# A two-layer hybrid decoder on one core: the instruction order taken from the scheduler's timeline model in place of its list model

## The chip, the cores and the metric

The kernel runs on one core of one Trainium2 chip. The metric is the device time of one execution in microseconds (us); the runs shown are of the same program on the same kind of chip, and the figure compared is their median. Matrix work runs on TensorE (PE in the profile, its weight loads PEld), elementwise work on VectorE (DVE), ScalarE (ACT) and GpSimd (POOL), and SyncE (SP) issues most DMAs.

## The reference

Two decoder layers over 512 tokens of width 1024, float32, each of them three residual steps with a layer norm behind each:

```
x <- LN(alpha*x + 0.5*SwiGLU_1(x))
x <- LN(alpha*x + W_o concat[DiffAttn | StickBreakingAttn | GatedDeltaNet](x W_in))
x <- LN(alpha*x + 0.5*SwiGLU_2(x))
```

The SwiGLU steps have a hidden width of 2816. The mixer in the middle has three parts: differential attention (4 heads, two softmaxes of 32-wide queries and keys each), stick-breaking attention (4 heads of 64, whose weights come from a reverse cumulative sum over the keys), and a gated delta rule (4 heads of 128). The delta rule cuts the sequence into chunks, solves a unit lower triangular system per chunk, and then carries a 128x128 state from chunk to chunk:

```
sol = lax.linalg.triangular_solve(t_mat, rhs, left_side=True, lower=True, unit_diagonal=True)
v_new = u_i - einsum(w_i, state)
out   = einsum(q_i * exp(g_i), state) + einsum(a_i, v_new)
state = state * exp(g_last) + einsum(k_i * exp(g_last - g_i), v_new)
```

## The kernel before, in words

Everything is held feature-major, 128 features on the partitions and the 512 tokens along the free axis. A projection is a sum over 8 (or 22) blocks of 128x128 weights. To keep float32 accuracy with a faster matmul, weights and activations are split into a high and a low part, and `mm3` (lines 100 to 107) issues three matmuls per block: L103 high by high, L104 high weights by low activations, L105 low weights by high activations. Such a matmul of 512 columns is the unit of the bulk work; it is called a *filler* below wherever it stands between the steps of a chain that is made of other, smaller instructions. Weights stream in eight blocks at a time (L81, tile `wraw`), and `Stream.get` makes the two parts on ACT (L89, `whi`) and on DVE or POOL (L90, `wlo`).

Per layer the program is `ffn`, `mixer`, `ffn`. Each of them ends in a layer norm: `Norm.add` gathers sums, L179 transposes them on PE, DVE computes the mean and the inverse deviation (`ln_yn`), and L206 transposes those back on PE, after which the next stage's inputs can be made.

The mixer is where many small chains meet:

- `project_v`, then for the four delta heads projections, convolution and products (L537 is the last of these on PE).
- `triangle(h)` for each head: L615 spreads the decay sums on PE, DVE and ACT make the lower triangle (L625), SP stores it to DRAM (L627); L630 and L633 make `intra`.
- `base`: SP loads the diagonal 16x16 blocks of all heads (L644), DVE inverts them in 30 dependent steps (L652, L654), and SP stores them (L655, L657) and loads them back as full tiles (L660 `XT`, L662 `inv`).
- `double(h)`: PE L670, ACT L672, PE L675, DVE L676, PE L679, ACT L680. It makes 32-wide inverted blocks of 16-wide ones.
- `join(h, m)` for m = 32 and 64: PE L690, ACT L693, PE L697, DVE L699, and for m = 32 PE L704 and ACT L705. Each step waits for the one ahead of it.
- `operands(h)`: PE transposes L710 and L715, DVE L712 and L717.
- `state`: for two pairs of heads and four chunks in turn `scan`: PE L725, DVE L727, PE L731, DVE L733, PE L738, DVE L741 or L744 (the new state), and the output on PE L749, L750 and ACT L792. The two pairs take turns, and a pair's next L725 needs its new state. `emit` and L776 finish two chunks.
- Attention, of small units: scores on PE (L878, L879, into tile `psc`, which has two buffers), softmax work on DVE and ACT (L915 to L938, L466), transposes L902, copy L904, values L907, and per pair of heads a closing normalization (L946 to L964) with transposes L970.
- The attention's queries and keys come from `project_qk` (L826 to L847): a 24-matmul projection, then SP DMAs (L846, `kqv<-kqv`) that lay the parts of each head out on the partitions that L878 reads.

All of it is written one stage after another. What stands beside what on an engine is not written by hand: the framework's scheduler takes the program's instructions and their dependencies, models the run, and emits one fixed order per engine. Each engine then executes its own list strictly in that order, so an instruction that waits holds up all that is behind it on that engine, SP's DMA issues included. The program gives a few hints (`g.after`, which adds an order between two instructions without a wait), and those stay. The core of the projection:

```
nc.tensor.matmul(out=out, lhsT=whi, rhs=xhi, start=first, stop=False)
nc.tensor.matmul(out=out, lhsT=whi, rhs=xlo, start=False, stop=False)
nc.tensor.matmul(out=out, lhsT=wlo, rhs=xhi, start=False, stop=last)
```

and one head's first half of `join` (a pair of blocks per corner):

```
nc.tensor.matmul(out=pt[hi, c, lo], lhsT=LTs[h][lo, c, hi], rhs=X[h][lo, c, lo], ...)
nc.scalar.copy(out=Y[hi, :, lo], in_=pt[hi, :, lo])
nc.tensor.matmul(out=pt[lo, c, hi], lhsT=Y[hi, c, lo], rhs=XT[h][hi, c, hi], ...)
nc.vector.tensor_tensor(out=XT[h][lo, :, hi], in0=XT[h][lo, :, hi], in1=pt[lo, :, hi], ...)
```

## Time and profile before

| what | value |
|---|---|
| time, three runs | 2253.29, 2254.13, 2255.03 us; median 2254.13 us |
| profiled execution | 2255.08 us, of which the profile's span is 2252.1 us |
| mean granted clock of TensorE | 0.978 |
| PE busy | 2141.5 us (95%) |
| PEld, DVE, ACT, POOL busy | 1792.2, 1153.2, 886.4, 346.7 us |
| HBM read, written | 189.64 MB, 6.83 MB |

The span runs from the first to the last recorded instruction; the 3.0 us between span and time lie around it. The profiled execution is 0.95 us above the median of the runs. Two layers follow one another: the first mixer lies between about 400 and 770 us, the second between about 1520 and 1890 us, and the rest is SwiGLU. A wait in the profile is idle time of an engine ahead of an instruction, with the instruction that released it. A granted clock of 1.00 stands for TensorE's level of 2.4 GHz, and 0.50 would be the level of 1.2 GHz throughout; a mean in between says how the stretch was shared between the two.

### The profile page before, as it was taken

Reading aid. Unit: us, or ns where it says so; the run is one execution under the profiler, and the core shown is the slowest. Engines: PE = TensorE matmul, PEld = TensorE weight load, DVE = VectorE, ACT = ScalarE, POOL = GpSimd, SP = SyncE. Lnnn points to the kernel's source line nnn. Section 1 sums busy time; section 2 is a strip of 40 time slices with the busy share of each in tenths; the row PEclk is TensorE's granted clock in tenths of the full one; section 3 lists DMA queues with packets and bytes.
Section 4 is the critical chain, followed back from the end, with each engine's and each line's share of the span. In section 5 each row is a group of like instructions: output and inputs, shape, how many; then the busy total and the mean of one; then the engine's idle time right before and its main releaser. Section 6 shows DMA issues by size and latency. Waiting matters only on the chain.

```text
span 2252.1 us, 29920 instructions
## 1 busy us (share of the span) xinstructions
PE 2141.5 (95%) x11382; PEld 1792.2 (80%) x11382; DVE 1153.2 (51%) x2347; ACT 886.4 (39%) x1755; POOL 346.7 (15%) x295
## 2 busy tenths in 40 slices
PE   8999999997988999999999999999989889999997
PEld 7888889876767888888888888898768668888886
DVE  4533436455687843333563334274566788333426
ACT  4333324545554533332443333155454635333313
POOL 1100011442113500000130000024511144000010
PEclk9999999999998999999999999999999889999998
DMA  6433323335221233332333333233442213333322
GB/s 186 128 94 97 97 75 104 94 97 135 76 67 47 84 104 100 96 94 75 113 103 96 100 94 94 66 104 103 113 101 76 76 48 103 94 95 100 96 66 94
DMA packets 89742, 213.08 MB, mean 95 GB/s; under 512 B 21840, under 2 KB 36208, under 8 KB 89600
## 3 DMA queue, kind: packets, MB, share of 16 engines
q1 hardware_dynamic: 81696, 183.27, 26.8%
q10 hardware_dynamic: 6912, 25.17, 3.7%
q0 software_dynamic: 992, 2.75, 0.7%
q8 instruction: 89, 1.46, 0.3%
q14 instruction: 53, 0.43, 0.1%
HBM read 189.64 MB, written 6.83 MB: 87 GB/s over the span
## 4 chain that ended last, share of the span: by engine, by line
PE 79%; DVE 12%; DMA 3%; ACT 2%; issue 2%; SPq 1%; POOL 1%; ACTq 0%; POOLq 0%; DVEq 0%
PE pd L104 23%; PE pd L103 23%; PE pd L105 23%; DMA wraw<-in_w 2%; DVE wlo L90 2%; PE po L907 1%; DVE x L212 1%; ACT whi L89 1%; DVE lt L166 1%; DVE at L937 1%; DMA kqv<-kqv 1%; PE psc L878 1%; DVE x L220 1%; PE pt L902 1%; DVE x L163 1%
## 5 line engine op out<-in xcount | busy, mean ns | idle before, releaser
L89 ACT CAST whi<-wraw 128x512 fp32r<-128x512 f32 x692 | 423.1, 620 | 990.8 <-PE pd L104 798.6
L90 DVE TENSOR_TENSOR wlo<-wraw,whi 128x512 fp32r<-128x512 f32 x580 | 431.0, 750 | 640.3 <-ACT whi L89 628.1
L103 PE MATMUL pd<-x,whi 128*128 128x512 f32 (+1 forms) x1888 | 714.6, 379 | 6.6 <-ACT x L1169 6.1
L104 PE MATMUL pd<-x,whi 128*128 128x512 f32 (+1 forms) x1888 | 715.6, 379 | 1.7 <-POOL x L231 1.1
L105 PE MATMUL pd<-x,wlo 128*128 128x512 f32 (+1 forms) x1888 | 713.3, 378 | 3.1 <-DVE wlo L90 3.1
L103 PEld LDWEIGHTS pd<-x,whi 128*128 128x128 f32 x1888 | 357.1, 190 | 70.9 <-ACT x L1169 6.1
L105 PEld LDWEIGHTS pd<-x,wlo 128*128 128x128 f32 x1888 | 357.6, 189 | 66.4 <-DVE wlo L90 3.3
L104 PEld LDWEIGHTS pd<-x,whi 128*128 128x128 f32 x1888 | 357.6, 189 | 66.3 <-POOL x L231 3.0
L103 PE MATMUL pd<-hhi,whi 128*128 128x512 f32 (+1 forms) x880 | 307.7, 350 | 0.0
L104 PE MATMUL pd<-hlo,whi 128*128 128x512 f32 (+1 forms) x880 | 307.6, 350 | 0.0
L105 PE MATMUL pd<-hhi,wlo 128*128 128x512 f32 (+1 forms) x880 | 307.2, 349 | 0.0
L90 POOL TENSOR_TENSOR wlo<-wraw,whi 128x512 fp32r<-128x512 f32 x112 | 151.9, 1360 | 297.8 <-ACT whi L89 214.2
L168 POOL TENSOR_TENSOR lt<-lt 128x512 f32<-128x512 f32 x26 | 39.2, 1509 | 1016.2 <-ACT lt L165 1012.1
L103 PEld LDWEIGHTS pd<-hhi,whi 128*128 128x128 f32 x880 | 165.4, 188 | 24.4
L105 PEld LDWEIGHTS pd<-hhi,wlo 128*128 128x128 f32 x880 | 165.4, 188 | 24.2
L104 PEld LDWEIGHTS pd<-hlo,whi 128*128 128x128 f32 x880 | 165.4, 188 | 24.1
L258 DVE TENSOR_TENSOR lt<-pd,lt 128x512 f32<-128x512 f32 x88 | 60.4, 690 | 112.6 <-PE pd L105 111.2
L134 POOL TENSOR_TENSOR x<-x 128x512 f32<-128x512 f32 x48 | 74.1, 1581 | 74.1 <-DVE ams L957 70.6
L515 DVE SCALAR_TENSOR_TENSOR kqv<-pd,conv,kqv 128x511 f32<-128x511 f32 (+2 forms) x54 | 40.3, 747 | 60.4 <-ACT kqv L513 59.4
L260 DVE TENSOR_TENSOR hlo<-lt,hhi 128x512 fp32r<-128x512 f32 x88 | 67.1, 765 | 6.2
L231 POOL TENSOR_TENSOR x<-x 128x256 fp32r<-128x256 f32 x60 | 45.9, 766 | 152.1 <-ACT x L229 148.3
L165 ACT ACTIVATE lt<-x 128x256 f32<-128x256 f32 (+1 forms) x58 | 29.5, 512 | 100.0 <-DVE x L163 99.8
(307 smaller groups left out, 2300.0 us busy)
## 6 DMA issues: line engine op xcount, KB each, us to landing
wraw<-in_w SPq DMA_DIRECT2D x300, 512.0 KB, 3.5
wraw<-in_w ACTq DMA_DIRECT2D x48, 512.0 KB, 3.6
kqv<-kqv SPq DMA_DIRECT2D x128, 64.0 KB, 2.0
kqv<-kqv SPq DMA_DIRECT2D x48, 128.0 KB, 3.8
scr<-zero POOLq DMA_DIRECT2D x2, 1032.0 KB, 11.4
x<-in_xT SPq DMA_DIRECT2D x8, 256.0 KB, 5.9
scr<-inv SPq DMA_DIRECT2D x8, 256.0 KB, 3.4
XT<-scr SPq DMA_DIRECT2D x8, 256.0 KB, 5.2
```

The source lines that it names most:

```text
L89: nc.scalar.copy(out=hi, in_=r)
L90: (eng or self.eng or nc.vector).tensor_tensor(out=lo, in0=r, in1=hi.bitcast(F32), op=ALU.subtract)
L103: nc.tensor.matmul(out=out, lhsT=whi, rhs=xhi, start=first, stop=False)
L104: nc.tensor.matmul(out=out, lhsT=whi, rhs=xlo, start=False, stop=False)
L105: nc.tensor.matmul(out=out, lhsT=wlo, rhs=xhi, start=False, stop=last)
L134: i = g.nc.gpsimd.tensor_tensor(out=t, in0=xhi.bitcast(F32), in1=xlo.bitcast(F32), op=ALU.add)
L165: nc.scalar.activation(out=sq[:, r], in_=t[:, r], func=AF.Square)
L168: eng.tensor_tensor(out=self.acc2[:, r], in0=self.acc2[:, r], in1=sq[:, r], op=ALU.add)
L231: eng.tensor_tensor(out=xlo[:, r], in0=t[:, r], in1=xhi[:, r].bitcast(F32), op=ALU.subtract)
L258: nc.vector.tensor_tensor(out=sg, in0=pu, in1=sg, op=ALU.mult)
L260: nc.vector.tensor_tensor(out=hlo, in0=sg, in1=hhi.bitcast(F32), op=ALU.subtract)
L515: nc.vector.scalar_tensor_tensor(out=y[:, s:], in0=p[:, :T - s], scalar=wc[:, 3 - s:4 - s], in1=y[:, s:], op0=ALU.mult, op1=ALU.add)
```

## The change

One argument is added where the kernel is built. The program, its tiles, its buffers and its hints stay as they are; the scheduler's model of the run, by which it chooses which instruction to emit next, is another.

```
-    with tile.TileContext(nc) as tc, ExitStack() as ctx:
+    with tile.TileContext(nc, schedule_with_timeline_sim=True) as tc, ExitStack() as ctx:
```

Both orders hold the same instructions. Of PE's 10860 instructions 4022 stand at another place, nearly all of them in the two mixers and around the layer norms; the bulk of the SwiGLU stages is in the same order. Three places follow, with the order of one engine before and after; "x8" behind a row stands for eight such instructions in a row.

**SP in the first mixer, around the stores and loads of `base`.** `scr_98` to `scr_100` are the three DRAM scratch tensors, `kqv<-kqv` the layout DMAs of L846. Before:

```order
L644 DMA blk<-scr_98 128x16x16
L846 DMA kqv<-kqv 64x512 x6
L655 DMA scr_99<-blk 128x16x16
L657 DMA scr_100<-blk 128x16x16
L846 DMA kqv<-kqv 64x512 x2
L660 DMA XT<-scr_99 128x4x128
L662 DMA inv<-scr_100 128x4x128
```

Behind these rows come the other three pairs of L660 and L662, and then four more L846 of this form. Now:

```order
L627 DMA scr_98<-inv 128x4x128
L644 DMA blk<-scr_98 128x16x16
L846 DMA kqv<-kqv 64x512 x5
L655 DMA scr_99<-blk 128x16x16
L657 DMA scr_100<-blk 128x16x16
L846 DMA kqv<-kqv 64x512 x2
L660 DMA XT<-scr_99 128x4x128 x2
L662 DMA inv<-scr_100 128x4x128 x2
```

Ahead of L644 there were 12 of the 24 L846 of this form, and there are 16 now; behind the last L662 there were four, and there is one.

**PE at the first joins of the first mixer.** `pd` with `x` is a projection's filler, `pa` the chain. Before, from the first L704 on:

```order
L704 MATMUL pa<-ident,XT 64x64 x4
L690 MATMUL pa<-inv 32x32 x8
L104 MATMUL pd<-x,whi 128x512
L105 MATMUL pd<-x,wlo 128x512
L103 MATMUL pd<-x,whi 128x512
L697 MATMUL pa<-XT,inv 32x32 x8
L104 MATMUL pd<-x,whi 128x512
L105 MATMUL pd<-x,wlo 128x512
L103 MATMUL pd<-x,whi 128x512
L704 MATMUL pa<-ident,XT 64x64 x4
```

Now, from the first L690 on:

```order
L690 MATMUL pa<-inv 32x32 x8
L907 MATMUL po<-kqv,at 128x64 x2
L902 MATMUL pt<-ident,at 128x128
L697 MATMUL pa<-XT,inv 32x32 x8
L704 MATMUL pa<-ident,XT 64x64 x4
L690 MATMUL pa<-inv 32x32 x8
L697 MATMUL pa<-XT,inv 32x32 x8
L704 MATMUL pa<-ident,XT 64x64 x4
L690 MATMUL pa<-inv 32x32 x8
```

Three fillers stood before nearly every L697 and L704. Now 19 stand in one row behind the last L690 shown, and of the twelve L697 and L704 of the eight joins seven follow directly on the PE step that they continue, three with one to four small matmuls of the attention between, and two with fillers; the four joins at m = 64 have no filler at all.

**PE at the scans of the first mixer.** Before, behind the second L725 (`S` is the state, `vn` the chunk's new values):

```order
L731 MATMUL pa<-inv,XT 128x128
L104 MATMUL pd<-x,whi 128x512
L105 MATMUL pd<-x,wlo 128x512
L103 MATMUL pd<-x,whi 128x512
L731 MATMUL pa<-inv,XT 128x128
L104 MATMUL pd<-x,whi 128x512
L105 MATMUL pd<-x,wlo 128x512
L103 MATMUL pd<-x,whi 128x512
L104 MATMUL pd<-x,whi 128x512
L738 MATMUL pa<-vn,inv 128x128 x2
```

Now, from the second L725 to the third:

```order
L725 MATMUL pa<-S,kqv 128x128 x2
L731 MATMUL pa<-inv,XT 128x128 x2
L738 MATMUL pa<-vn,inv 128x128 x2
L749 MATMUL pa<-S,kqv 128x128
L750 MATMUL pa<-vn,intra 128x128
L749 MATMUL pa<-S,kqv 128x128
L750 MATMUL pa<-vn,intra 128x128
L725 MATMUL pa<-S,kqv 128x128 x2
```

Between the first L725 and the L731 of the fifth one there stood 35 fillers; there is none now. They stand earlier: 24 of them between the steps of the two pairs' first chunks, the others, of the projection tile before, among the joins. In the same way the second, third and fourth `triangle` start 22, 33 and 46 places further down on PE: behind L537 there are 87 fillers ahead of the fourth L615 where there were 41, and 172 ahead of the first L670 where there were 144. Between these two there are 85 now and were 103. At the layer norms behind a SwiGLU stage the first L206 stands 48 places further down.

## Rows read from the trace of the kernel before

**Rows 1.** The page's first part: busy time, share and instructions of each engine.

```profile
PE 2141.5 (95%) x11382; PEld 1792.2 (80%) x11382; DVE 1153.2 (51%) x2347; ACT 886.4 (39%) x1755; POOL 346.7 (15%) x295
```

**Rows 2.** Windows: one SwiGLU stage and the two mixers; the first row names the columns.

```profile
core 0: us, PE busy (x) PEld busy (x) DVE busy (x) ACT busy (x) POOL busy (x), PEclk, DMA share, GB/s
1150.00:1450.00 300.00, 300.00 (x1303) 244.42 (x1303) 116.64 (x169) 94.45 (x158) 12.26 (x9) 1.00 0.31 95
400.00:700.00 300.00, 269.48 (x1621) 218.28 (x1621) 182.01 (x481) 156.52 (x367) 84.85 (x67) 0.94 0.32 88
1520.00:1820.00 300.00, 270.10 (x1617) 218.41 (x1615) 185.50 (x487) 155.25 (x366) 87.69 (x69) 0.94 0.32 88
```

**Rows 3.** Windows: shorter stretches of the first mixer.

```profile
480.00:560.00 80.00, 66.17 (x365) 53.52 (x364) 49.46 (x129) 39.72 (x94) 29.29 (x24) 0.96 0.53 134
540.00:560.00 20.00, 12.76 (x62) 10.01 (x63) 2.76 (x4) 7.40 (x18) 1.94 (x1) 0.84 0.63 166
580.00:620.00 40.00, 40.00 (x387) 31.13 (x387) 23.09 (x62) 17.40 (x49) 5.12 (x4) 1.00 0.39 102
613.00:634.00 21.00, 20.95 (x139) 17.79 (x138) 17.75 (x74) 6.21 (x17) 0.00 (x0) 1.00 0.05 12
660.00:680.00 20.00, 11.42 (x55) 9.26 (x54) 14.53 (x43) 10.95 (x28) 0.00 (x0) 0.65 0.42 132
```

**Rows 4.** Waits of PE over the whole span: in total, times, longest.

```profile
PE psc L878 <- DMA kqv<-kqv: 14.8, 6, 3.8
PE pa L206 <- DVE ln_yn L116: 14.4, 10, 3.6
PE pt L970 <- DVE at L964: 13.5, 4, 4.4
```

**Rows 5.** Timeline of PE at the first `triangle` and `double`: start, duration, idle before.

```profile
500.25 0.60 PE L615 MATMUL pa<-ident,G 128*128 128x128 f32 x4
...
541.45 0.41 PE L878 MATMUL psc<-kqv 128*128 128x384 f32 x1 [2.38 <-DMA kqv<-kqv]
...
544.41 0.94 PE L670 MATMUL pa<-inv,lt 128*128 128x128 f32 x6 [0.45 <-DMA inv<-scr]
...
554.12 1.51 PE L878 MATMUL psc<-kqv 128*128 128x384 f32 x3 [3.78 <-DMA kqv<-kqv]
```

**Rows 6.** Timeline of PE, ACT and DVE at one join of the first mixer.

```profile
585.20 0.44 PE L690 MATMUL pa<-inv 32*32 32x32 f32 x16
585.57 0.50 PE L104 MATMUL pd<-x,whi 128*128 128x512 f32 x1
...
586.48 0.44 PE L697 MATMUL pa<-XT,inv 32*32 32x32 f32 x16
...
587.74 0.41 PE L704 MATMUL pa<-ident,XT 64*64 64x64 f32 x4
...
585.70 0.54 ACT L693 COPY inv<-pa 32x128 f32<-32x128 f32 x2
...
586.96 0.59 DVE L699 TENSOR_TENSOR XT<-XT,pa 32x128 f32<-32x128 f32 x2 [2.30 <-PE pa L697]
```

**Rows 7.** Timeline of PE and DVE at the scans of the first mixer.

```profile
613.01 0.71 PE L725 MATMUL pa<-S,kqv 128*128 128x128 f32 x4
...
635.17 0.68 PE L731 MATMUL pa<-inv,XT 128*128 128x128 f32 x4 [0.54 <-DVE inv L727]
...
634.67 0.61 DVE L727 SCALAR_TENSOR_TENSOR inv<-pa,neG,inv 128x128 f32<-128x128 f32 x2 [1.46 <-PE pa L725]
635.89 0.42 DVE L733 TENSOR_TENSOR vn<-pa,brk 128x256 f32<-128x256 f32 x1 [0.61 <-PE pa L731]
...
632.60 0.60 DVE L744 SCALAR_TENSOR_TENSOR S<-S,eG,pa 128x128 f32<-128x128 f32 x2 [0.81 <-PE pa L738]
```

## The prediction

> **What bounds the kernel now.** I read the page's busy times first, then windows, then PE's waits, then the timeline where the order changes. The page shows PE busy for 95% of the span [rows 1]; 2252.1 less 2141.5 us leaves 110.6 us in which PE has nothing to do. The windows say where those lie. A SwiGLU stage is busy for 300.00 of 300 us at clock 1.00, with 1303 matmuls at 300/1303 = 0.230 us [rows 2]; its order is the same in both kernels, so nothing is to be had or lost there. The two mixers are busy for 269.5 and 270.1 of 300 us at a mean clock of 0.94 [rows 2]: they hold 60 of the 110.6 us, and both show the same picture, so I work out the first mixer and double it. Most of the rest lies at the layer norms.
>
> The shorter windows of the mixer split it again [rows 3]. From 480 to 560 us (`triangle`, `base`, the first `double`) PE idles for 13.8 us, 7.2 of them after 540, where the clock also sinks to 0.84. From 580 to 634 us (joins and scans) it idles for practically nothing: 40.00 of 40, 20.95 of 21. From 660 us on, at the end of the attention, it idles again for 8.6 of 20 us at clock 0.65. The wait list names the releasers: scores waiting for the layout DMAs, 14.8 us in six waits; the norms' return, 14.4; the attention's L970, 13.5 [rows 4].
>
> So the old order is bad around `double` and nearly perfect in the joins and scans. The new one does the opposite in both places.
>
> **The change part by part, per mixer.** All work stays; what changes is which chain stands uncovered.
>
> *1. `triangle` comes later: +1.0 us.* The fourth L615 starts at 500.25 and the first L670 at 544.41 us [rows 5], 44.2 us apart; between them lie a store and two rounds through DRAM and the 30 dependent DVE steps of `base`, which no order on PE shortens. With 87 instead of 41 fillers ahead, it stands 46 x 0.23 = 10.6 us lower; the first `triangle` stands 16 mostly short instructions higher, some 1.9 us, so I take 8.7 us later. By the first L670 28 more fillers are done, 28 x 0.23 = 6.4 us, which are saved later. 8.7 - 6.4 = 2.3 us is the upper end. If the 18 fillers fewer inside the chain shorten it by up to 2.7 us, it comes to -0.4. I take +1.0, nearer the middle.
>
> *2. The stalls around `double` go: -6.8 us.* The scores at 541.45 and 554.12 wait 2.38 and 3.78 us for layout DMAs, and L670 waits 0.45 for its tile [rows 5]: 6.6 us. On SP those layout DMAs stand behind the stores and loads of `base`; in the new order three more of the last four, and all of the earlier ones, stand ahead of the loads, and 39 fillers stand between the first L670 and the first L679 where there were 3. The clock of 0.84 over 20 us [rows 3] is 3.2 us of TensorE pulses not granted. Together 9.8 us, if both go. About 3 us should stay, since the second L670's tile still comes over the same loads and scores with two buffers still wait for DVE: -6.8, bounds -9.8 and 0.
>
> *3. The joins lose their cover: +5.5 us.* L690 starts at 585.20; ACT's two copies run from 585.70 for 0.54 us each to the next, so that L697 could start at about 586.3; it starts at 586.48, because three fillers of 0.23 us fill the gap [rows 6]. L697 to L704 is alike over DVE: 586.96 plus 0.59, then 587.74 [rows 6]. Start to start a bare hop takes 1.1 us, 0.35 of it the matmuls themselves: 0.75 us idle. Seven hops are bare now, 5.3 us, and three have a few small matmuls, say 0.35 left, 1.0 us: 6.3. At m = 64 there is one copy instead of two, so I take 5.5. Upper end 7.0 (with the operands behind them, where the fillers thin out too), lower end 0, if the attention's waits would have cost the same time anyway.
>
> *4. The scans lose theirs: +6.2 us.* From 613.01 to 634 us PE is full at clock 1.00 [rows 3]; 35 fillers lie there, 35 x 0.23 = 8.0 us, and now none. Bare hops can be read where the old order has them so: DVE takes 0.61 us for L727 and L731 waits [rows 7]; L725 to L731 is about 1.25 us start to start, of which 0.45 is matmul. L731 to L738 over L733 (0.42 us, ending at 636.31 [rows 7]) is about 1.2, again 0.45 of it matmul. The new state (L744, 0.60 us [rows 7]) is hidden behind the other pair's step. So a bare step idles for 0.8 + 0.75 = 1.55 us; four of them, 6.2. Bounds: 0, if the attention's scores cover them in practice, and 8.0, all that was filled there.
>
> **The Trainium skill, "Perfetto Trace Analysis", § Optimization Strategy,** holds that a kernel whose most-contended engine changes from regime to regime may gain from interleaving the regimes. By it alone this change would cost, for it takes projections out from between joins and scans; with steps 3 and 4 only, the sum would be 2 x 11.7 = 23 us worse. The rows agree for the old order (40.00 of 40 us busy in the joins), but the rule does not say that the same fillers pay elsewhere, which is step 2.
>
> *5. Attention in lumps: +1.0 us.* The stick-breaking units run from the third `triangle` to `double` with few fillers, and the doubles of heads 1 to 3 have attention between their hops in place of fillers. By the hop of rows 6 up to three half-covered hops, 2 us; 0 if the attention covers them. I take half.
>
> *6. Layer norms: -1.0 us for the whole kernel.* L206 waits 14.4 us in ten places, 3.6 at the longest [rows 4]. Behind the SwiGLU stages it stands 48 places later, so some of these waits are filled; at most about a third, 4.5 us. At the mixers' norms it stands some 35 to 40 places later too but the tiles behind it are reordered and start later, which may cost 0.5 to 2 us each.
>
> **Sum.** Per mixer 1.0 - 6.8 + 5.5 + 6.2 + 1.0 = +6.9; twice that is 13.8, less 1.0 is +12.8 us. 2255.08 + 12.8 = 2267.9 us against the profiled execution, which stands 0.95 above the median: **2267 us**, 0.6% slower.
>
> **The rivals.**
>
> *A. Faster: the fillers moved up pay more than they cost.* The place is 480 to 560 us, where 13.8 us idle [rows 3]. If the 28 fillers done earlier sit in these gaps, step 2 brings its full 9.8, step 1 its -0.4, and the joins and scans are covered by attention units whose DVE and ACT work now comes earlier, so that 3 and 4 together cost only 3: -7.2 per mixer, with step 6 -15.4 in all, 2255.08 - 15.4 - 0.95 = 2239 us. It decides from the point where joins and scans together lose less than the 6.8 of step 2. For it: the waits of the attention are the largest item on the list [rows 4]. Against it: 7 bare hops and 4 bare steps can be counted in the order.
>
> *B. No change.* Steps 3 and 4 come to about half, 5.8, and cancel 2 with 1: 2254 us. That the change does nothing is excluded, 4022 PE instructions move, but that cover is only shifted is possible.
>
> *C. Much slower: the clock.* The old order shows that low occupancy goes with a lower clock: 12.76 of 20 us busy at 0.84, 11.42 of 20 at 0.65, while the joins and scans, filled, have 1.00 [rows 3]. A bare join is 0.35 of 1.1 us busy, a bare scan step about 2.3 of 3.8, and both come in a row. If each costs as much clock as the stretch from 540 us, 3.2 us twice per mixer, the sum grows by 13 to 2280; with a loss like that from 660 us (0.35 x 20 = 7 us) in one of them, to about 2287.
>
> The Trainium skill, "TensorE: Matmul & The Clock Gate", § What's actually happening, says that TensorE is throttled by default and that activity releases it. The trace agrees as far as it goes (0.65 where PE is half idle); by that rule alone C would be the likeliest case, but half-busy stretches with many small matmuls are not shown in these rows.
>
> **How the numbers follow.** My forecast (2259 to 2275) gets 0.38, C 0.22, together 0.60 for slower. A gets 0.26. B gets 0.14. Under 0.2%, 4.5 us, a measurement of this kernel can't tell a difference from none. The range takes in most of A and C: 2240 to 2287, of which the forecast's own is 2259 to 2275. The unknown ends of steps 2 to 4 (-9.8 to 0, 0 to 7.0, 0 to 8.0) would reach further on either side, all at once only.
>
> **What would show it.** Right: in the new profile the waits of L878 on layout DMAs shrink to under half of 14.8 us; L697, L704, L731 and L738 appear among the waits with a total of about 10 us per mixer; the window that holds the joins and scans is busy for about 80%, with the SwiGLU windows at 100% as before. Wrong: if L697 and L731 show little waiting, step 3 or 4 is oversized and A or B holds; if L878's waits stay, step 2 failed and it is slower still; if the clock in the joins or scans reads well under 1.00, C holds. The fourth L615 should start some 9 us later, and the first L670 likewise, or step 1 is off.

## The result, and the profile after

The changed kernel takes **2305.61 us** (median of four runs, 2303.30 to 2306.38) against 2253.71 us for the kernel before (median of four runs): a ratio of 1.0227, 95% interval 1.0211 to 1.0242. It is slower, as forecast, but by 52 us and not by 13, and the time lies above the range of 2240 to 2287 us.

The first part of the page of the changed kernel answers to [rows 1]; its span is 2301.6 us.

```profile
PE 2169.2 (94%) x11382; PEld 1827.5 (79%) x11382; DVE 1145.1 (50%) x2347; ACT 887.0 (39%) x1755; POOL 343.5 (15%) x295
```

PE idles for 2301.6 - 2169.2 = 132.4 us where it idled for 110.6: 21.8 of the 49.5 us by which the span grew. The other 27.7 us are PE being busy for longer with the same 11382 instructions. The mean granted clock fell from 0.978 to 0.957. So more than half of the loss is not waiting at all. The bulk of a SwiGLU stage is untouched, full at clock 1.00, as in [rows 2]:

```profile
1200.00:1460.00 260.00, 260.00 (x1129) 212.01 (x1128) 98.67 (x147) 82.03 (x136) 3.02 (x3) 1.00 0.31 97
```

Next, the waits of PE over the whole span, which answer to [rows 4] (in total, times, longest):

```profile
PE pd L103 <- DVE x L163: 15.4, 2, 7.8
PE pa L206 <- DVE ln_yn L116: 13.5, 3, 5.0
PE pd L103 <- ACT x L228: 13.3, 6, 3.1
PE po L907 <- ACT at L904: 10.2, 12, 2.5
...
PE pa L776 <- DVE o L771: 8.7, 2, 4.3
...
PE pa L738 <- DVE vn L733: 4.7, 9, 0.6
PE pa L731 <- DVE inv L727: 4.2, 8, 0.5
...
PE pa L697 <- ACT inv L693: 3.8, 7, 0.9
...
PE psc L878 <- DMA kqv<-kqv: 2.3, 2, 1.2
```

The scores' wait for layout DMAs is down from 14.8 to 2.3 us, and the joins' and scans' steps (L697, L731, L738) are in the list as foretold, but small. At its head stand waits where the sum had no loss: at the layer norms (L163 and L206, and L228, with which a norm makes the next stage's inputs) and at the end of the attention (L907, L776).

To see where the time went I cut the mixer at events that both kernels have: the first L537, the first L670, the last L679, the last L710, the fifth L725, the first matmul of the output projection, the last L970, and 10 us behind the last L206. Windows of the kernel before, first mixer (columns as in [rows 2]):

```profile
481.08:544.41 63.33, 54.85 (x310) 44.36 (x308) 47.40 (x127) 33.76 (x82) 26.80 (x23) 1.00 0.51 127
544.41:579.38 34.97, 28.21 (x177) 23.83 (x178) 18.10 (x35) 19.18 (x43) 5.20 (x3) 0.90 0.28 71
579.38:606.01 26.63, 26.63 (x296) 19.61 (x295) 10.63 (x26) 11.17 (x33) 5.28 (x5) 1.00 0.40 106
606.01:633.92 27.91, 27.86 (x188) 23.95 (x187) 23.60 (x87) 9.64 (x25) 0.00 (x0) 1.00 0.19 49
633.92:684.83 50.91, 40.07 (x239) 33.55 (x239) 37.41 (x125) 34.12 (x95) 5.65 (x6) 0.82 0.29 83
684.83:704.94 20.11, 14.91 (x51) 10.29 (x50) 17.23 (x37) 10.03 (x24) 8.94 (x6) 0.79 0.08 22
704.94:768.69 63.75, 57.12 (x411) 53.18 (x412) 53.45 (x117) 30.42 (x64) 25.59 (x22) 0.97 0.19 60
```

The same seven stages of the changed kernel:

```profile
481.30:551.45 70.15, 66.14 (x331) 55.32 (x330) 50.99 (x128) 36.38 (x85) 31.00 (x25) 0.88 0.58 147
551.45:579.54 28.09, 27.40 (x194) 24.13 (x193) 17.95 (x37) 20.15 (x47) 5.63 (x5) 1.00 0.25 74
579.54:612.88 33.34, 28.96 (x279) 22.25 (x279) 13.99 (x40) 9.93 (x29) 0.00 (x0) 0.74 0.18 44
612.88:643.39 30.51, 24.44 (x156) 20.10 (x157) 21.62 (x70) 7.53 (x19) 0.00 (x0) 1.00 0.11 28
643.39:703.56 60.17, 44.62 (x240) 37.35 (x239) 41.85 (x128) 34.43 (x98) 5.54 (x6) 0.74 0.25 71
703.56:724.33 20.77, 19.10 (x85) 15.28 (x83) 13.44 (x34) 9.46 (x22) 10.89 (x6) 0.94 0.09 27
724.33:792.75 68.42, 52.16 (x361) 49.78 (x362) 51.63 (x116) 30.09 (x63) 25.66 (x24) 0.85 0.18 54
```

The first mixer with its norm grew by 23.8 us and the second, cut alike, by 21.7; together 45.5 of the 49.5 us. Fillers were moved between stages, so a stage's change has to be set off against them, at 0.23 us each as in the prediction; what is left is the price of the order:

| stage | change, first / second mixer | fillers | net of fillers | predicted |
|---|---|---|---|---|
| L537 to L670 (`triangle`, `base`) | +6.8 / +7.5 | +28, 6.4 us | +0.4 / +1.1 | +1.0 (step 1) |
| L670 to L679 (`double`) | -6.9 / -6.9 | +15, 3.5 us | -10.4 / -10.4 | -6.8 (step 2) |
| L679 to L710 (joins) | +6.7 / +4.4 | -23, 5.3 us | +12.0 / +9.7 | +5.5 (step 3) |
| L710 to fifth L725 (scans) | +2.6 / +1.7 | -20, 4.6 us | +7.2 / +6.3 | +6.2 (step 4) |
| fifth L725 to output projection | +9.3 / +10.0 | 0 | +9.3 / +10.0 | not in the sum |
| output projection and norm | +5.3 / +5.1 | 0 | +5.3 / +5.1 | gain (step 6) |

One of the 28 fillers of the first row stands directly ahead of the first L537 in the new order, so that its 0.23 us lie outside the window. The table compares two traces, and one of its stages differs between executions of the same order: in the fifteen traces of this document that have the old order up to the last L679, `double` took 28.0 to 35.7 us over their thirty mixers, 33.9 at the median, and the trace of the kernel before, with 34.97, is at the long end. Against that median the net gain of `double` is 9.3 us and not 10.4. Unedited joins and scans vary by 0.1 us, and the stage from the fifth L725 to the output projection took 50.7 to 51.9 us in every trace that leaves its old order as it is.

### The profile page after: what moved, and what is told of

The parts are those of the page before. It is cut to its first block, busy times and chain, and to the rows that moved or that the text cites. A ratio compares the mean times of both kernels' runs of the same rounds, so it can differ in the third digit from the quotient of the medians.

```text
span 2301.6 us, 29925 instructions
## 1 busy us (share of the span) xinstructions
PE 2169.2 (94%) x11382; PEld 1827.5 (79%) x11382; DVE 1145.1 (50%) x2347; ACT 887.0 (39%) x1755; POOL 343.5 (15%) x295
## 4 chain that ended last, share of the span: by engine, by line
PE 85%; DVE 7%; issue 3%; ACT 2%; DMA 2%; POOL 0%; SPq 0%; ACTq 0%; POOLq 0%
PE pd L104 24%; PE pd L103 24%; PE pd L105 24%; DMA wraw<-in_w 2%; PE po L907 2%; PE pt L902 1%; PE psc L878 1%; DVE wlo L90 1%; DVE x L212 1%; PE psc L104 1%; PE psc L103 1%; PE psc L105 1%; DVE x L220 1%; ACT at L466 1%; ACT whi L89 0%
## 5 line engine op out<-in xcount | busy, mean ns | idle before, releaser
L89 ACT CAST whi<-wraw 128x512 fp32r<-128x512 f32 x692 | 420.2, 620 | 971.8 <-PE pd L104 783.8
L90 DVE TENSOR_TENSOR wlo<-wraw,whi 128x512 fp32r<-128x512 f32 x580 | 423.4, 739 | 652.2 <-ACT whi L89 646.5
L103 PE MATMUL pd<-x,whi 128*128 128x512 f32 (+1 forms) x1888 | 706.2, 381 | 19.6 <-ACT x L228 13.3
L104 PE MATMUL pd<-x,whi 128*128 128x512 f32 (+1 forms) x1888 | 714.0, 380 | 4.7 <-POOL x L231 3.2
L103 PEld LDWEIGHTS pd<-x,whi 128*128 128x128 f32 x1888 | 356.2, 192 | 86.6 <-ACT x L228 15.4
L104 PEld LDWEIGHTS pd<-x,whi 128*128 128x128 f32 x1888 | 360.8, 191 | 74.1 <-POOL x L231 6.6
L104 PE MATMUL pd<-hlo,whi 128*128 128x512 f32 (+1 forms) x880 | 308.1, 350 | 0.0
L103 PE MATMUL pd<-hhi,whi 128*128 128x512 f32 (+1 forms) x880 | 307.4, 349 | 0.0
L103 PEld LDWEIGHTS pd<-hhi,whi 128*128 128x128 f32 x880 | 165.5, 188 | 24.4
L104 PEld LDWEIGHTS pd<-hlo,whi 128*128 128x128 f32 x880 | 165.5, 188 | 24.3
L90 POOL TENSOR_TENSOR wlo<-wraw,whi 128x512 fp32r<-128x512 f32 x112 | 149.4, 1340 | 228.5 <-ACT whi L89 194.0
L134 POOL TENSOR_TENSOR x<-x 128x512 f32<-128x512 f32 x48 | 73.0, 1568 | 88.0 <-DVE kqv L993 88.0
L165 ACT ACTIVATE lt<-x 128x256 f32<-128x256 f32 (+1 forms) x58 | 29.3, 512 | 105.8 <-DVE x L163 93.6
L907 PE MATMUL po<-kqv,at 128*128 128x64 f32 x320 | 59.8, 332 | 10.7 <-ACT at L904 10.2
L231 POOL TENSOR_TENSOR x<-x 128x256 fp32r<-128x256 f32 x60 | 45.5, 762 | 161.5 <-ACT x L229 100.2
```

Of the source, the lines that this page charges most:

```text
L89: nc.scalar.copy(out=hi, in_=r)
L90: (eng or self.eng or nc.vector).tensor_tensor(out=lo, in0=r, in1=hi.bitcast(F32), op=ALU.subtract)
L134: i = g.nc.gpsimd.tensor_tensor(out=t, in0=xhi.bitcast(F32), in1=xlo.bitcast(F32), op=ALU.add)
L165: nc.scalar.activation(out=sq[:, r], in_=t[:, r], func=AF.Square)
L231: eng.tensor_tensor(out=xlo[:, r], in0=t[:, r], in1=xhi[:, r].bitcast(F32), op=ALU.subtract)
L907: nc.tensor.matmul(out=po[:, col:col + 64], lhsT=wT[:, ch(k)], rhs=V[k][:, vc:vc + 64], start=k == 0, stop=k == qt)
```

## The experiments

For the experiments the order of each engine was pinned, instruction by instruction, by order edges that carry no wait, so that the same program can be run with any order between the two. "The tail" is the stage from the fifth L725 to the output projection; "the norm" is output projection and layer norm behind the mixer.

**1. The change in parts.** Each of these kernels takes the new order on all engines in one region of both mixers and the old one elsewhere. In short form:

```
e1_front   new | old tail | old norm
e1_tail    old | new tail | old norm
e1_norm    old | old tail | new norm
```

> The new order everywhere but from the fifth L725 of each mixer to the end of its layer norm, where the old order stands. Theory P (each part costs by itself what the traces show there): in the traces the fifth L725 of the first mixer is 9.5 us late, that of the second 7.4 us later than its own start, and the SwiGLU norms add about 1, so +17 to +19 us, about 2272. Rival Q (the fillers spent early are what is missing later, so the parts behind are late whatever their order): nearly the whole of +52, 2300 or more. Rival R (the front is neutral, the end of the attention and the norm cost all): under +5, 2259 or less.

> The old order everywhere but from the fifth L725 of each mixer to the first matmul of the output projection (the end of the scans and of the attention), where the new order stands. Theory P: the traces show this part 9 to 10 us longer in each mixer, so +18 to +20 us, about 2273. Rival Q: within 5 us of before, since the fillers ahead of it are where they were. Rival R: +25 or more.

> The old order everywhere but from the first matmul of the output projection to the last L206 of each mixer's norm, where the new order stands. Theory P: the traces show this part 5 to 6 us longer in each mixer, so +10 to +12 us, about 2265. Rival Q: within 3 us of before. Rival R: +20 or more. The three parts together make the whole change: by P their sums add up to about +47 to +52.

Against 2256.01 us: the front alone 2279.36 us (ratio 1.0113, 1.0083 to 1.0143), the tail alone 2269.71 (1.0069, 1.0042 to 1.0097), the norm alone 2267.31 (1.0053, 1.0032 to 1.0074). That is +23.4, +13.7 and +11.3, together 48.4 of 52: within the intervals, of some 5 to 7 us on either side for each part, the parts add, and none of them is a gain. The front costs rather more than the +17 to +19 that were expected of it, the tail rather less than its +18 to +20. The front, where all of steps 1 to 5 lie, is less than half of the whole. Its trace also shows what the old tail does behind the new front, which has spent its fillers early:

```profile
646.54:697.46 50.92, 40.36 (x239) 33.72 (x239) 37.38 (x125) 34.14 (x95) 5.64 (x6) 0.81 0.28 83
```

That is the 50.91 us of the kernel before; in the second mixer it is 51.9. So the tail's cost comes from its own order.

**2. Bare joins and bare scans, each by itself.** Old order; on PE the 40 fillers between the joins are moved behind the last join, or the 35 between four scan steps behind those; a few instructions of other engines (L81, L89, L832 and L833 at the joins, L727 and L744 at the scans) follow. The number of fillers in each stage stays. The edit at the second join:

```
 L690 MATMUL pa<-inv 32x32 x8
-L104 MATMUL pd<-x,whi 128x512
-L105 MATMUL pd<-x,wlo 128x512
-L103 MATMUL pd<-x,whi 128x512
 L697 MATMUL pa<-XT,inv 32x32 x8
-L104 MATMUL pd<-x,whi 128x512
-L105 MATMUL pd<-x,wlo 128x512
-L103 MATMUL pd<-x,whi 128x512
 L704 MATMUL pa<-ident,XT 64x64 x4
```

> The old order with one edit in each mixer: the 40 fillers among the joins stand behind them, ahead of the first L710. Step 3 of the prediction alone: +5.5 us per mixer, +11 in all, about 2267 (0 to +14). Theory K (an uncovered stretch costs its idle time and, on top, the time that PE then works at the lower clock): idle about 6 us per mixer between the first L690 and the first L710, a clock of 0.6 to 0.85 there, and +7 to +10 us per mixer, +14 to +20. Rival: the fillers given back right behind the joins take the place of other waits, and it costs under 2 us per mixer.

> The old order with one edit in each mixer: the 35 fillers between the first and the fifth L725 stand behind the four steps. Step 4 of the prediction alone: four bare steps at 1.55 us, +6.2 us per mixer, +12.4 in all, about 2268 (0 to +16). Theory K as read from the new order's trace, where a bare hop waits 0.53 us and not 0.78 and the clock stays at 1.00: 8 hops at 0.53, +4.2 us per mixer, less what the attention's scores cover there, so +5 to +8 in all, and a clock of 1.00 in the scans.

The bare joins cost 2274.07 against 2253.96 us (1.0091, 1.0073 to 1.0109), the bare scans 2263.99 (1.0054, 1.0034 to 1.0074). Windows of the two stages, the joins' in the first kernel and the scans' in the second:

```profile
578.48:616.49 38.01, 32.93 (x297) 26.39 (x296) 10.59 (x26) 11.32 (x33) 5.30 (x5) 0.73 0.23 59
```

```profile
600.89:635.03 34.14, 29.66 (x188) 25.15 (x187) 23.39 (x87) 11.08 (x28) 0.00 (x0) 1.00 0.15 40
```

The scans: 34.14 - 27.91 = 6.2 us, the figure of step 4, at clock 1.00, and as much in the second mixer. (This trace as a whole took 2258.36 us, less than the median, since `double`, which the edit does not touch, took 29.8 and 28.0 us in it.) The joins idle for 38.01 - 32.93 = 5.1 us, close to the 5.5 of step 3, but the stage grew by 11.4: PE was busy for 6.3 us longer with the same instructions, at clock 0.73. The timeline of PE in that kernel shows how:

```profile
582.58 0.41 PE L704 MATMUL pa<-ident,XT 64*64 64x64 f32 x4 [0.37 <-DVE XT L699]
...
584.86 0.63 PE L704 MATMUL pa<-ident,XT 64*64 64x64 f32 x4 [0.37 <-DVE XT L699]
...
589.31 0.92 PE L697 MATMUL pa<-XT,inv 32*32 32x32 f32 x16 [0.41 <-ACT inv L693]
...
601.12 0.63 PE L104 MATMUL pd<-x,whi 128*128 128x512 f32 x1
601.55 0.63 PE L105 MATMUL pd<-x,wlo 128*128 128x512 f32 x1
...
605.39 0.39 PE L105 MATMUL pd<-x,wlo 128*128 128x512 f32 x1
605.62 0.40 PE L103 MATMUL pd<-x,whi 128*128 128x512 f32 x1
```

L704 takes 0.41 us at its first run in the stage and 0.63 at the next; L697 takes 0.92, where [rows 6] have 0.44. After the last join the fillers at first start 0.43 us apart, and from 605.39 on 0.23: for some 5 us more PE works at the lower of the clock's two levels, with no wait any more. In the changed kernel the 19 fillers behind the last L690 shown in the order begin the same way:

```profile
586.43 0.63 PE L104 MATMUL pd<-x,whi 128*128 128x512 f32 x1
586.86 0.63 PE L105 MATMUL pd<-x,wlo 128*128 128x512 f32 x1
...
590.08 0.40 PE L104 MATMUL pd<-x,whi 128*128 128x512 f32 x1
590.31 0.40 PE L105 MATMUL pd<-x,wlo 128*128 128x512 f32 x1
```

**3. The order up to the first L670 alone**, new on every engine, old behind it: in place of step 1.

```
 fillers from L537:  to first L670   to last L679   joins   scans
 before                    144            29           47      44
 e6_first                  172             1           47      44
```

The 172 take in the one directly ahead of the first L537.

> Order of the change on every engine up to the first L670 of each mixer, old order behind it; 28 projection matmuls more than before stand ahead of the first L670, and only 1 instead of 29 between it and the last L679. Theory K (step 1 was wrong in what it credits: the chain from the fourth L615 to L670 does not become shorter with fewer fillers in it, it only becomes barer, and the clock falls there): L537 to the first L670 takes 69 to 71 us at a clock of 0.86 to 0.90, as in the changed kernel, and was 63 us at 1.00; the fourth L615 to L670 stays at 44 us. The stage from the first L670 to the last L679, with 28 fillers fewer and the early layout DMAs, is 27 to 29 us instead of 35, so that the whole is within 0.1% to 0.3% of the kernel before (2 to 6 us slower). Theory S (step 1 as predicted): L537 to L670 64 to 66 us, and the whole faster, by 8 to 12 us, as in the kernel with SP's order alone mended.

2256.99 against 2254.55 us (1.0008, 0.9997 to 1.0020): no difference that can be told. Its first two stages:

```profile
483.19:553.35 70.16, 66.18 (x332) 55.40 (x330) 51.03 (x128) 35.38 (x83) 30.21 (x24) 0.88 0.57 147
553.35:578.97 25.62, 18.86 (x146) 16.18 (x145) 16.43 (x33) 17.28 (x38) 1.27 (x1) 1.00 0.05 12
```

Theory K came out: 70.2 and 71.5 us, the next stages even shorter than it said (25.6 and 27.0), the whole within its range, and the fourth L615 to L670 at 44.3 us in the first mixer (44.2 before), so the chain is no shorter with fewer fillers in it, and the clock falls. Yet the net price of step 1 is small, as in the sum: 28 fillers are 6.4 us, and the stage costs 0.4 us beyond them in the first mixer and 2.3 in the second. Theory S's gain did not come: the layout DMAs are early here too, but `double` without its fillers idles for 6.8 of 25.6 us.

**4. One queue alone.** Old order; on SP the four L846 that stood behind all loads of `base` go behind the first pair:

```
 L660 DMA XT<-scr_99 128x4x128
 L662 DMA inv<-scr_100 128x4x128
+L846 DMA kqv<-kqv 64x512 x4
 L660 DMA XT<-scr_99 128x4x128
...
-L846 DMA kqv<-kqv 64x512 x4
```

> The old order with one edit on SP in each mixer: the four layout DMAs (L846) that stand behind all eight L660 and L662 are put behind the first pair, ahead of the other three. This is step 2 of the prediction by itself, without moving any filler. In the old order the score at 554 us waits 3.8 us for one of these DMAs, which is issued at 545.8 though its source is there before 538. Theory (that wait is SP's order): it goes or falls under 1 us, the clock ahead of L679 with it is near 1.00, and the part from the first L670 to the last L679 is 4 to 7 us shorter in each mixer: 6 to 12 us faster than before. Rival (the loads of the other heads come later by as much and L670 waits for them, or the DMA engines are full there anyway): within 3 us of before.

**2242.61 against 2253.43 us, ratio 0.9948 (0.9932 to 0.9963): faster than both kernels.** The waits of PE's scores on layout DMAs fall from 14.8 us [rows 4] to

```profile
PE psc L878 <- DMA kqv<-kqv: 6.4, 4, 2.4
```

and `double` takes 27.97 us in place of 34.97, at clock 0.99 (28.2 in the second mixer):

```profile
543.84:571.81 27.97, 25.32 (x179) 21.37 (x178) 17.29 (x35) 19.45 (x44) 4.56 (x3) 0.99 0.28 80
```

Against the median of 33.9 us of the unedited `double` that is 5.9 and 5.7 us, and the runs are 10.8 us faster. So more than half of the 9.3 us that `double` gains in the new order can be had from one queue, without moving a filler.

**5. The tail.** First, only PE's new order there (the other engines free to follow). In the old order a projection's 24 last fillers stand in eight groups of one to eight among the attention's units; in the new one they stand in two rows, of 21 and 3:

```
 L902 MATMUL pt<-ident,at 128x128 x4
+L103, L104, L105 MATMUL pd<-x 128x512 x21
 L750 MATMUL pa<-vn,intra 128x128
```

> The old order, with PE's new order in the end of scans and attention and no order set for the other engines there (the old list model places them around PE's). Theory O (PE's order makes the part longer, whatever VectorE and ScalarE do): as that part alone with all engines, +11 to +17 over before. Rival (the order of VectorE and ScalarE in the new list, with their short operations between the attention's, is the cause): under +5.

2269.36 against 2253.49 us (1.0071, 1.0047 to 1.0095), as much as the whole tail's new order: PE's own order is enough to cost it. Three runs then asked whether it is where the row stands, by putting it elsewhere: behind the last chunk's L750 in the changed kernel; and, in the kernel with the tail alone, all 24 ahead of the second L776, or behind values and scores.

> The new order with one edit in each mixer: the 21 fillers between the L749 and the L750 of the last chunk stand behind them. Theory P1 (the lump holds back the last scan's output, and L776, which waits 4.33 us in the first mixer for what is made of it, holds back the attention): that wait goes, and half to all of the 9 to 10 us of this part with it, so 9 to 18 us faster than the new order, 2288 to 2297. Rival (the attention's own chains over DVE and ACT set the end of this part anyway, and the wait turns up at the scores and L970 instead): within 3 us of the new order, 2303 to 2307.

> The kernel with the new order in the end of scans and attention alone, and in it the 24 fillers of the projection whose first 21 stand behind the L749 of the last chunk put directly ahead of the second L776, which waits 4.3 us. Theory P1 (the lump holds back the last scan's output and, through VectorE's order, the attention's scores, by 5 us): 8 to 14 us faster than that part alone, so +0 to +6 over before, and the wait at L776 gone. Rival (the part's length is the attention's own chain over DVE and ACT in the new order, wherever the lump stands): within 3 us of that part alone, +11 to +17 over before.

> The kernel with the new order in the end of scans and attention alone, and in it PE's 21 and 3 fillers behind the last L749, L750, the values and the scores that followed them, directly ahead of the next L902; all other engines keep the new order. Theory P6 (the 21 fillers stood ahead of everything that VectorE and ScalarE had to work on; with that work released first they cover it): ScalarE's wait for L750 of 4.4 us goes and the kernel is 5 to 10 us faster than that part alone, +3 to +8 over before. Rival (the attention's chain is as long either way, and what is gained ahead is lost behind, as with the two edits of this part before): within 3 us of that part alone, +11 to +17.

2306.62 against 2256.01 (1.0234, 1.0206 to 1.0261), 2274.09 against 2253.96 (1.0094, 1.0077 to 1.0110), 2272.81 against 2253.49 us (1.0088, 1.0063 to 1.0114). None gives anything back; the tail measured 59.9 to 61.4 us in the last two, and 60.2 in the changed kernel. A fourth run took away its longest single wait, L776's 4.3 us, whose inputs DVE made late; on ACT the casts L992 and copies L984 went behind L779:

```
-L992 CAST kqv<-x 128x256 x2
...
 L779 ACTIVATE x<-pa,dng 128x256 x2
-L992 CAST kqv<-x 128x256 x2
...
-L984 COPY kqv<-pd 128x512 x2
...
 L779 ACTIVATE x<-pa,dng 128x256 x2
+L992 CAST kqv<-x 128x256 x4
+L984 COPY kqv<-pd 128x512 x2
```

> The kernel with the new order in the end of scans and attention alone, and in it four L992 and two L984 of ScalarE, which the new order puts ahead of the last L779, put directly behind it, as in the old order; the 21 fillers stay where the new order has them. Theory P3 (these L992 release GpSimd's L993 and L134 early, and while GpSimd runs those, VectorE's short operations L111 to L116 for L771 take 0.65 to 1.2 us each in place of 0.16 to 0.2; L776 waits 4.3 us for L771 and the attention with it): L114 and L116 back to 0.2 us there, the wait at L776 gone or under 1 us, and 6 to 10 us faster than that part alone, +3 to +8 over before. Rival (the filler lump's 5 us set the length, VectorE catches up): within 3 us of that part alone, +11 to +17 over before.

2271.54 against 2253.95 us (1.0068, 1.0042 to 1.0093): no better. L776's longest wait fell to 1.2 us, but the tail took 58.96 us in the first mixer and 59.4 in the second, where the tail alone had 60.0 and 60.1: PE idles for some 1.8 us less there and is busy for longer, at clock 0.72 where it was 0.74.

```profile
PE pa L776 <- DVE o L771: 2.5, 2, 1.2
```

```profile
633.23:692.19 58.96, 45.43 (x239) 37.76 (x239) 39.30 (x127) 34.30 (x97) 6.16 (x6) 0.72 0.25 72
```

What fits all five runs: the tail is a chain of softmax units that PE, ACT and DVE pass to one another, and the old order's fillers lay inside its waits. In a row, at any of four places, they are work beside which that chain does not advance. Idle time rose from 10.8 to 15.6 us, by 4.7; 24 fillers are 5.5. The rest of the 9.3 us is the clock, 0.74 after 0.82. This reading is argued, not shown: the old tail takes 50.9 us behind the old front and behind the new one, but its small steps, too, stand a little differently (in the new order the last chunk's L731 stand behind two more scores, L878), and no run has the new order of the small steps with the 24 fillers spread as before.

**6. The norm.** Again only PE's new order first:

> The old order, with PE's new order in output projection and norm and no order set for the other engines there. Theory O: as that part alone with all engines, +8 to +14 over before. Rival (VectorE's row of L162 and what stands behind it is the cause, PE's order is harmless with VectorE's old way): under +4.

2266.92 against 2253.49 us (1.0061, 1.0043 to 1.0078): again PE's order is enough. Between the first matmul of the output projection and the last L970 it has 72 fillers where there were 39, so 33 fewer are left behind L970, where the norm's chain runs. In the changed kernel the timeline of PE behind L970 has two large waits:

```profile
746.62 0.58 PE L103 MATMUL pd<-kqv,whi 128*128 128x256 f32 x1 [7.63 <-DVE x L163]
...
768.08 0.66 PE L206 MATMUL pa<-ident,ln_yn 128*128 128x128 f32 x2 [4.98 <-DVE ln_yn L116]
```

Four runs on top of the kernel with the norm alone tried to take these apart: DVE's seven L162 taken out of their row and each put ahead of its own L163; L155 moved up; both; and one tile's 24 fillers moved ahead of another's.

```
-L162 SCALAR_TENSOR_TENSOR x<-x,lt 128x512 x7
+L162 SCALAR_TENSOR_TENSOR x<-x,lt 128x512
 L158 COPY lt<-x 128x512
 L163 TENSOR_TENSOR x<-pd,x 128x512
+L162 SCALAR_TENSOR_TENSOR x<-x,lt 128x512
 L163 TENSOR_TENSOR x<-psc,x 128x512
```

> The kernel with the new order in output projection and norm alone, and in it VectorE's seven L162, which stand in a row ahead of the first L163, each put directly ahead of its own L163, as in the old order; PE keeps the new order. Theory P2 (that row of 6.4 us keeps the PSUM tiles, so that PE waits 7.6 us for L163): that wait falls by 4 to 6 us and the kernel is 6 to 10 us faster than that part alone, +1 to +5 over before. Rival (PE's order is the cause: the four first tiles end later and L155 stands 33 places behind the first of them): within 3 us of that part alone, +8 to +14 over before.

> The kernel with the new order in output projection and norm alone, and in it one PE instruction per mixer moved: L155, the mean of the first tile, from 33 fillers behind that tile to 9 behind it; L162 stays in a row. Theory P4 (VectorE's run from L157 to the sums that L179 waits for is 19.4 us in both orders, and L157 starts 4 us later after L151, since L155 is late on PE): L179 and L206 come 3 to 5 us earlier in each mixer, 6 to 9 us faster than that part alone, +2 to +5 over before. Rival (the row of L162, or the end of the four first tiles behind another tile's 22 fillers, sets it): within 3 us of that part alone, +8 to +14 over before.

> The kernel with the new order in output projection and norm alone, and in it both earlier edits together: each L162 directly ahead of its L163, and L155 moved up to 9 fillers behind its tile. Theory P7 (two delays side by side, the late L155 and the row of L162; either alone hides behind the other): L163's and L206's waits fall together and 6 to 10 us of the 11 go, +1 to +5 over before. Rival (the first four tiles end late, behind another tile's 22 fillers, and the rest follows from that): no more than 4 us faster than that part alone, +7 or more.

> The kernel with the new order in output projection and norm alone, and in it one edit on PE per mixer: the 24 fillers of the tile that belongs to the first half of the tokens (L163's seventh) stand ahead of the 20 fillers of a second-half tile, as in the old order, and not behind them. Theory P8 (the first half's sums, L179 and L206, wait for that tile): L179 and L206 come 2 to 4 us earlier in each mixer and 4 to 8 us of the 11 go, +3 to +7 over before. Rival (both tiles wait for a PSUM tile that L163 frees, so their order is the same to it): within 3 us of that part alone, +8 to +14.

2261.97 against 2253.96 (1.0035, 1.0019 to 1.0051), 2261.31 against 2253.95 (1.0031, 1.0020 to 1.0043), 2263.37 against 2253.49 (1.0049, 1.0030 to 1.0068), 2266.61 against 2253.43 us (1.0062, 1.0042 to 1.0081). The first halves the wait at L163 (15.2 to 8.0 us), and the norm's window is still 69.3 us where the old order has 63.75; in the second, the first mixer's `double`, which the edit does not touch, took 29.3 us where the norm alone had 33.3, as much as its whole lead. None of the four edits removes the cost: +8.0, +7.4, +9.9 and +13.2 us after the +11.3 of the norm alone, and what the first two seem to save is within the intervals. That the 33 fillers used up ahead of L970 are missing behind it is argued from the windows (idle 5.2 to 1.7 us ahead of it, 6.6 to 16.3 behind), not shown by a run that puts back just these; which of them matter stays open.

**7. A gap of the old order.** In the old order L970 waits for 13.5 us in all [rows 4]. On DVE the weight splits L90 that stand in its chain were put behind L964.

```
-L90 TENSOR_TENSOR wlo<-wraw,whi 128x512
 L116 SCALAR_TENSOR_TENSOR af<-arr_t,af 128x8
-L90 TENSOR_TENSOR wlo<-wraw,whi 128x512
...
 L964 TENSOR_TENSOR at<-at,af 128x512
-L90 TENSOR_TENSOR wlo<-wraw,whi 128x512 x4
+L90 TENSOR_TENSOR wlo<-wraw,whi 128x512 x7
```

> The old order with one edit in each mixer: at the two closing normalizations of the differential attention VectorE's L90 that stand between L951 and L964 (three and one) are put behind L964. In the old order PE waits 4.4 and 2.3 us there for L964 through L970. Theory (PE's wait is VectorE's own order, and nothing needs these weight parts sooner): these waits fall by about 2.0 and 0.7 us, 2 to 3 us per mixer, 4 to 6 us faster than before, and the clock behind them higher. Rival (what L90 makes is late then, and PE waits as long for it, L105 or L103 behind L90): within 2 us of before.

2256.24 against 2253.95 us (1.0012, 1.0001 to 1.0023): no gain. L970's longest wait falls from 4.4 to 3.1 us, and two waits of 4.8 appear at the step behind it:

```profile
PE pt L902 <- ACT x L973: 9.6, 2, 4.8
```

## Why the prediction missed

**Step 1 (later `triangle`, +1.0) held.** L615 and L670 came 6.9 and 7.0 us later, where some 9 were foretold; with 28 fillers done, +0.4 and +1.1 net. Experiment 3 shows the same: no difference in all.

**Step 2 (the stalls around `double`, -6.8) held and was too small.** The net gain was 10.4 us against the trace of the kernel before, a little more than the upper bound of 9.8, and 9.3 against the median of the old order's traces. The scores' waits on layout DMAs fell to 2.3 us, and the clock is back at 1.00. About 3 us were held back for L670's loads and DVE; that caution was hardly borne out. Experiment 4 shows that SP's order alone carries more than half of it.

**Step 3 (the joins, +5.5) is the first term that was mis-sized.** Its idle time was right: 4.4 us in the changed kernel, 5.1 in experiment 2. But a hop was priced at the clock of the filled stage (0.44 us for L697), and bare joins run at the lower one for much of their time (mean clock 0.74 and 0.84 in the two mixers): net 12.0 and 9.7 us, 7.6 and 5.4 beyond the idle time. This is the mechanism of rival C in the place it named, and larger than its 3.2 us.

**Step 4 (the scans, +6.2) was right,** 6.2 us in isolation, 7.2 and 6.3 net in the changed kernel. Rival C expected the clock to sink here too; it reads 1.00 in every trace.

**Step 5 (attention in lumps, +1.0) was the wrong place for that cost.** It was sought between `triangle` and `double`. It lies in the tail, for which the sum has no term, and the prediction gives no reason why none was needed, though it had itself read the end of the attention as idle for 8.6 of 20 us at clock 0.65. No filler leaves that stage, and the steps of chain and attention there are in nearly the same order; mostly the fillers' place among them differs, and the new order costs 9.3 and 10.0 us per mixer. This missing term is the largest single error.

**Step 6 (layer norms, -1.0 for the kernel) has the wrong sign.** The step itself named the mixers' norms, "which may cost 0.5 to 2 us each", and let the SwiGLU norms outweigh them; measured, output projection and norm cost 5.3 and 5.1 us per mixer, 11.3 in the run by itself. Nor did the SwiGLU norms gain: outside the mixers and their norms the span grew by 4.0 us. Ahead of the first mixer and between the mixers the waits of L206 and L179 are gone (1.7 and 4.3 us before), as foretold, but L103 and L104 wait there for L228 and L231 instead, for 3.2 and 5.1 us.

**The sum.** It was +12.8 us; the span grew by 49.5. Of the 36.7 us that are missing, the tail is 19.3, the norms 15.4 (10.4 at the mixers' and 4.0 elsewhere in place of -1.0), the joins 10.7 and the scans 1.1, less 7.2 that step 2 gave on top and 2.6 of steps 1 and 5.

**The signs foretold.** L878's waits shrank to under half: right. L697, L704, L731 and L738 about 10 us per mixer in the wait list: about 8 us. Joins and scans busy for about 80%: (28.96 + 24.44) / (33.34 + 30.51) = 84%. "If the clock in the joins or scans reads well under 1.00, C holds": 0.74 in the joins. All of these tests looked at the three places that the sum knew, and none at the two that decided.

**The rivals.** A failed where its own condition said: joins and scans cost more than step 2 brought, and the attention covered neither. B needed joins and scans at 5.8 us per mixer; they came to 17.7. C's price of 13 to about 20 us on top of the sum was too low, since the clock sank in places that it did not name as well: 0.88 from L537 to L670 (1.00 before), 0.74 in the tail (0.82), 0.85 at the norm (0.97).

The rule cited from the Trainium skill, "Perfetto Trace Analysis", § Optimization Strategy, that interleaving regimes may pay, points the right way here: experiment 1's front and both kernels of experiment 2 are losses by un-interleaving. The 23 us worked out by it for the joins and scans alone was nearer to the result than my sum, though it came out so for another reason, since those two net +35 us in both mixers and `double` gives 21 of them back.

## What to carry to other kernels

When a scheduler's option reorders a tuned kernel, cut both orders at common events and count for every stage the filler work that enters, leaves or only changes its place; price the stage as fillers moved, plus idle time of the bare hops, plus the clock, and leave no stage out, however alike its steps look. Look at where filler work stands as well as at how much there is: here 24 fillers in one or two rows, at any of four places, won back nothing of what the old order has with the same 24 spread over a chain that passes between engines. Where the new order has one real gain (here a few DMA issues behind loads on SP's queue), make that one move by itself.

## What the runs showed of the hardware

**The clock does not follow idle time alone.** Bare joins idle for 5.1 of 38.0 us and run at 0.73, with no single wait above 0.8 us; bare scans idle for 4.5 of 34.1 and run at 1.00; `double` of experiment 3 idles for 6.8 of 25.6 at 1.00 (and for 6.7 of 27.0 at 0.94 in the second mixer). The joins' matmuls are 32x32 and 64x64, the scans' 128x128; whether that is what decides was not tried. The Trainium skill, "TensorE: Matmul & The Clock Gate", § What's actually happening, has the throttled level as the default, which activity releases; the trace agrees in that fillers in one row, at 0.43 us each, got the clock back to 0.23.

**VectorE's short operations stretched while GpSimd worked.** In the tail of the changed kernel DVE's chain towards L771 ran beside two GpSimd operations:

```profile
652.15 0.16 DVE L114 TENSOR_TENSOR orr_t<-of 128x4 f32<-128x4 f32 x1
...
662.42 1.19 DVE L116 SCALAR_TENSOR_TENSOR of<-orr_t,of 128x4 f32<-128x4 f32 x1
663.64 1.18 DVE L114 TENSOR_TENSOR orr_t<-of 128x4 f32<-128x4 f32 x1
664.86 0.16 DVE L115 SCALAR_TENSOR_TENSOR orr_t<-orr_t,oms 128x4 f32<-128x4 f32 x1
```

```profile
660.68 1.69 POOL L993 TENSOR_TENSOR kqv<-x,kqv 128x256 fp32r<-128x256 f32 x2 [0.87 <-DMA kqv<-kqv]
662.33 2.48 POOL L134 TENSOR_TENSOR x<-x 128x512 f32<-128x512 f32 x2
```

The same 128x4 operation took 0.16 us at 652.15 and 1.18 at 663.64, inside L134's 2.48 us, and 0.16 again once that had ended. The Trainium skill, "GPSIMD Engine Reference", § 1. Specifications, says that GpSimd's way into SBUF is shared with VectorE, with contention for VectorE instructions that run in a two-port mode or have two SBUF inputs; these rows, with two inputs each, agree. In experiment 5's run with L992 and L984 put later, GpSimd starts behind that chain, and all of the chain's operations take 0.15 to 0.17 us:

```profile
650.04 0.16 DVE L114 TENSOR_TENSOR orr_t<-of 128x4 f32<-128x4 f32 x1
```

```profile
654.73 2.78 POOL L993 TENSOR_TENSOR kqv<-x,kqv 128x256 fp32r<-128x256 f32 x4 [49.62 <-PE pt L902]
```

That run was no faster, so the stretching is not what the tail's cost hangs on.
